# The input projection's weights in two passes instead of four: a hybrid DeltaNet / S5 / HGRN2 layer on one core

## The chip, the cores and the metric

One Trainium2 chip; the kernel runs on one of its cores. The metric is the device time of one execution in microseconds (us), the median of several executions. A core has five engines with queues of their own: TensorE (PE, matmuls; PEld are its weight loads), VectorE (DVE), ScalarE (ACT), GpSimd (POOL) and SyncE (SP, which here issues most DMAs).

## The reference: what is computed

One layer of a hybrid network, in float32, on 2048 prompt tokens and 64 sample tokens (8 sequences of 8), model width 1024:

```python
hn = rmsnorm(h, norm_mix[i])
z = hn @ w_in[i]
z_qkv, z_gate, z_beta, z_a, z_u, z_hq, z_hf, z_hi, z_hg = jnp.split(z, IN_SPLITS, axis=-1)
qkv, buf_qkv = causal_dwconv(z_qkv, conv_qkv[i], dn_conv_w[i])
qkv = jax.nn.silu(qkv).reshape(bsz, t, 3, DN_HEADS, DN_HEAD_DIM)
...
o_a, s_delta = gated_delta_chunked(q, k, v, g, beta, delta[i])
...
y_b, x_re, x_im = s5_ssm(z_u, ssm_re[i], ssm_im[i], ssm_lam_re[i], ssm_lam_im[i], ssm_log_step[i],
...
o_c, s_hg = hgrn2_chunked(hq, hk, hv, jnp.log(f).reshape(hshape), hgrn[i])
...
h = h + jnp.concatenate([o_a, o_b, o_c], axis=-1) @ w_out[i]
hn = rmsnorm(h, norm_ffn[i])
up, buf_ffn = causal_dwconv(hn @ ffn_w_up[i], conv_ffn[i], ffn_conv_w[i])
a_ff, b_ff = jnp.split(up, 2, axis=-1)
h = h + (jax.nn.silu(a_ff) * b_ff) @ ffn_w_down[i]
```

The delta rule works in chunks of 64 tokens with a triangular solve, HGRN2 in chunks of 32 with a state passed from chunk to chunk, S5 is a diagonal scan. A gate, a small projection and a last norm follow; the states are outputs too.

## The kernel before

**Dense products.** Each float32 operand is split into a high part and a low remainder, and one product becomes three matmuls (hi·hi, lo·hi, hi·lo; `mm3`). The tokens are worked in four groups: 512 tokens each, the last one with the 64 sample tokens as well (576). Tiles of 128 tokens are numbered 0 to 15, the sample tile is 16. For each tile `norm_tiles` makes the norm (tile `nx`), transposes it on TensorE and splits it into `hnh` and `hnl` (ScalarE and VectorE); the pair of a group has one of two places, so group 2 takes that of group 0.

**Phase 1**, the input projection (`phase1`), goes group by group. First comes the token unit: for each tile 128 x 264 products for the columns that are wanted by tokens (`tok`). Then come 24 units, one for each block of 128 columns: 12 of qkv, 2 hf, 2 hq, 2 u, 4 zg, 2 hg. A unit is 24 matmuls, 8 steps of 128 rows with three each. It is emptied by `p1_evac`: for qkv two ScalarE copies (`raw`, and `y` with the last tap) and three VectorE steps `y<-raw,cw,y` of the convolution, then a silu on ScalarE and a store.

**The feed** (`Feed`) brings the weights of these units in order: each operand is loaded in two halves (`wr`, by SP), copied by ScalarE to `wh` (the high part) and subtracted to `wl` by GpSimd or VectorE (`split`, whichever is free earlier by the plan). `wh` and `wl` have three places each. `p1_feed` lists for each of the four groups the two token operands and the 24 blocks, so the whole of `w_in` is loaded and split four times, 104 operands.

**Background.** The delta rule (`delta_gen`), S5 and HGRN (`other_gen`) and the norms are Python generators that a class `Background` steps between the dense matmuls (`tick`). When a dense unit needs something that isn't made yet (`need`, `feed.get`), steps are taken by force until it is there. A class `Pace` keeps an estimate of when each engine is free; it only sets the order in which instructions are written. The order on each engine is thereby fixed when the kernel is built. `other_gen` is serial: HGRN of group 0 (two halves of 256 tokens), S5 of groups 0 and 1, HGRN of group 1, HGRN of group 2, S5 of groups 2 and 3, HGRN of group 3. HGRN of a group waits for its token unit and its hf, hq and hg blocks. A half group of HGRN is a load of its rows (`hw`), six doubling levels of small matmuls, transposes, four rounds over chunks with the state `SH`, a norm, and a store to `oT`.

**Phase 3**, the output projection (`phase3`), loads tiles of the mixed outputs back from `oT` as operands of the same feed (`wr<-oT`, split to `wh` and `wl`) against `w_out`, which `load_wo` splits into `woh` and `wol` in the places of the `hn` pairs that are done with. It is called twice; the first part (3a) has tiles 0 to 7, and tile i needs the delta rule, S5 and HGRN of its group. Then come the up projections of the feed-forward part for two groups at a time (phase 4), and the rest. Dense units are numbered through the program: 0 to 136 are phase 1 (group 3's blocks and token tiles count as more than one), and 137 is the first tile of phase 3a.

All instructions are issued by the wrapper `call` of `Pace.Engine`, so every row of the profile has line 71, and rows are told apart by the names of their tiles.

Of the kernel before, what the change touches and what calls it, by code (L numbers as in the profile page):

```python
# [9 lines left out]
F32 = mybir.dt.float32  # L10
# [23 lines left out]
# ranks of background work; how long (us) work of the first rank is waited for; the lead of VectorE over GpSimd  # L34
# [9 lines left out]
class Pace:  # L44
    """An estimate of when each engine gets through what it was given, in microseconds. It serves only to choose the
    order in which independent work is given to the engines."""
# [70 lines left out]
    def keys(ap):  # L117
        """The parts of a tile that ap touches, of those that work goes on in apart."""
# [17 lines left out]
    def ring(self, pool, tag, bufs, ap):  # L136
        """ap takes the place of the tile bufs before it."""
# [65 lines left out]
    def slot(self, what, t, d):  # L203
        """The end of the first gap of d from t on among what is planned."""
# [45 lines left out]
class Background:  # L250
    """Work that runs between the units of the dense products, a step of each at a time, when what the step before
    gave to the engines is done."""
# [8 lines left out]
    def add(self, gen, rank=5):  # L261
        """Generators of the lowest rank come first, and among equals those added first."""
# [4 lines left out]
    def step(self, gen):  # L267
        """The banks that a step of gen took; None when it could not be taken, False after the last."""
# [12 lines left out]
    def tick(self, budget=3, force=False):  # L281
# [13 lines left out]
        if force and not moved:  # L295
            # the first of all before others hold the engines up, then what is ready first
# [8 lines left out]
    def run(self, gen, done):  # L305
        """Steps of gen until done()."""
# [9 lines left out]
class Feed:  # L316
    """The stationary operands of the dense products in the order of their use, loaded and split ahead of it by halves."""

    W = KB * 132

    def __init__(self, m):
        self.m, self.items, self.made, self.raw = m, [], {}, {}
        self.loaded, self.next, self.cur, self.half = 0, 0, 0, None
# [40 lines left out]
    def ahead(self, n):  # L364
        """Steps to the first n operands."""
# [6 lines left out]
    def using(self, i):  # L372
        """Operands before i are in no more use."""
# [4 lines left out]
    def pump(self):  # L378
        """The next step when it holds nothing up."""
# [4 lines left out]
        elif self.next in self.raw and self.next // 2 <= self.cur + 2:  # L384
# [5 lines left out]
    def late(self):  # L390
        """Whether the splits come late and the engines that make them have work to go through."""
        nc = self.m.nc
        lead = {e: nc.free.get(e, 0.0) - nc.now() for e in ("vector", "scalar", "gpsimd")}
        return self.next < 2 * self.cur + 3 and (max(lead["vector"], lead["scalar"]) > 2 or lead["gpsimd"] > 3)

    def get(self, i):
        while self.next < 2 * i + 2:
# [47 lines left out]
class Model:  # L445
# [24 lines left out]
    def split(self, hi, lo, src, lo_eng=None):  # L470
        """hi + lo = src exactly, each in the form that one pass of the tensor engine carries."""
# [32 lines left out]
    def add_rows(self, out, ps, n, x):  # L504
        """out = x + the products of mm_rows."""
# [4 lines left out]
    def rsqrt(self, out, x, n, w, add=0.0):  # L510
        """out = (x + add) ** -0.5 for positive x + add of [n, w], by Newton steps; y takes the other sign in each."""
# [13 lines left out]
    def claim(self, n):  # L525
        """Steps until n of the five banks may be kept from step to step."""
# [12 lines left out]
    def room(self, n):  # L539
        """Steps until a single step may take n banks."""  # L540
# [22 lines left out]
    def masks(self):  # L563
# [11 lines left out]
        # the same within the sequences of the sample tile  # L575
# [17 lines left out]
    def row_bcast(self, dst, src):  # L593
        """A row of DRAM to every partition."""
# [4 lines left out]
    def norm_tiles(self, tiles, source, gain, place, mark, more=(), after={}):  # L599
        """Two generators for the split of (rmsnorm(rows) * gain) transposed, for (tile, group, off, n) of tiles: the  # L600
# [2227 lines left out]
```

## Time and profile before

| | us |
|---|---|
| median of 3 runs (3251.98 to 3255.48) | 3254.16 |
| span of the profiled execution | 3254.1 |
| PE busy | 3086.7 |
| VectorE busy | 1948.4 |
| ScalarE busy | 1246.1 |
| GpSimd busy | 1053.8 |

The span is what the profiler recorded of one execution from its first to its last instruction. An engine's busy time is the sum over its own instructions; the engines work beside each other, so the busy times don't add up to the span. The granted clock (PEclk) is the mean of what TensorE was allowed in a stretch as a share of 2.4 GHz; its lower level is 1.2 GHz. Projection products are `mm`, small background ones `mx`. Phase 1 ends at about 1016 us.

### The profile page before, as it was taken

The page shows a single profiled execution, that of the slowest core. Times are in us where ns is not written, and L with a number is a line of the kernel's source. Part 1 is how long each engine was busy: PE and PEld are TensorE (multiplying, and loading weights), DVE is VectorE, ACT ScalarE, POOL GpSimd, SP SyncE. Part 2 cuts the span into 40 slices and gives each one's busy share as a digit, 9 for nine tenths or more (in the row PEclk, how much of TensorE's full clock was granted, in tenths as well). Part 3 has the DMA queues.
Part 4 walks back from the last instruction along what each step waited for, and adds up shares of the span by engine and source line. Part 5 has one row for each costly group of instructions (what it writes and reads, how often), then busy time and mean ns, then how long its engine had stood idle before and what let it go on. Part 6 is the DMA issues. An engine that isn't in the chain of part 4 may idle for free.

```text
span 3254.1 us, 49953 instructions
## 1 busy us (share of the span) xinstructions
PE 3086.7 (95%) x17872; PEld 2554.5 (78%) x17872; DVE 1948.4 (60%) x4190; ACT 1246.1 (38%) x2920; POOL 1053.8 (32%) x1417
## 2 busy tenths in 40 slices
PE   8898898898898997999999999999999999999998
PEld 6676677687887776777677888999998888888886
DVE  8848859667857579766664446454555323323665
ACT  5454335445453433443243324333334223213333
POOL 4553423534535333134553315343331000000111
PEclk9899999998999998999999999999999999999999
DMA  6465573775467733754242333222225445544221
GB/s 176 132 176 146 140 211 98 203 223 158 130 172 201 224 97 99 202 169 113 80 131 72 97 120 117 63 70 70 67 67 159 135 126 164 148 124 133 73 88 56
DMA packets 627536, 425.52 MB, mean 131 GB/s; under 512 B 112613, under 2 KB 553833, under 8 KB 627016
## 3 DMA queue, kind: packets, MB, share of 16 engines
q1 hardware_dynamic: 596344, 384.24, 41.8%
q10 hardware_dynamic: 30944, 38.09, 3.4%
q8 instruction: 141, 2.31, 0.3%
q14 instruction: 107, 0.88, 0.1%
HBM read 302.69 MB, written 118.95 MB: 130 GB/s over the span
## 4 chain that ended last, share of the span: by engine, by line
PE 59%; DVE 5%; issue 1%; ACT 1%; DMA 1%; POOL 0%; SPq 0%; DVEq 0%; ACTq 0%; POOLq 0%
PE mm L71 53%; PE mx L71 7%; DVE y L71 2%; DVE b L71 1%; DVE R L71 1%; DVE rs L71 1%; DVE s5v L71 0%; SPq L71 0%; DMA b<-xs 0%; DVE s5t L71 0%; ACT djunk L71 0%; POOL s5o L71 0%; ACT y L71 0%; DMA Q<-dNN 0%; DMA dKV<-R 0%
## 5 line engine op out<-in xcount | busy, mean ns | idle before, releaser
L71 PE MATMUL mm<-hnh,wh 128*128 128x512 f32 (+2 forms) x2720 | 994.6, 366 | 20.7 <-ACT wh L71 18.8
L71 PE MATMUL mm<-hnh,wl 128*128 128x512 f32 (+2 forms) x2720 | 992.3, 365 | 17.5 <-POOL wl L71 15.0
L71 PE MATMUL mm<-hnl,wh 128*128 128x512 f32 (+2 forms) x2720 | 993.5, 365 | 0.0
L71 POOL TENSOR_TENSOR wl<-wr,wh 128x512 fp32r<-128x512 f32 (+1 forms) x396 | 564.5, 1434 | 619.8 <-ACT wh L71 604.9
L71 DVE SCALAR_TENSOR_TENSOR y<-raw,fw,y 128x512 f32<-128x512 f32 (+1 forms) x440 | 409.8, 939 | 364.2 <-ACT y L71 290.1
L71 PEld LDWEIGHTS mm<-hnh,wh 128*128 128x128 f32 x2720 | 524.2, 193 | 99.1 <-ACT wh L71 22.6
L71 PEld LDWEIGHTS mm<-hnh,wl 128*128 128x128 f32 x2720 | 523.3, 192 | 98.2 <-POOL wl L71 21.0
L71 PEld LDWEIGHTS mm<-hnl,wh 128*128 128x128 f32 x2720 | 523.5, 192 | 74.7 <-issue 4.9
L71 ACT ACTIVATE wh<-wr 128x512 fp32r<-128x512 f32 (+1 forms) x434 | 265.5, 631 | 161.4 <-PE mm L71 92.1
L71 ACT ACTIVATE raw<-mm 128x512 f32<-128x512 f32 (+3 forms) x336 | 154.8, 461 | 382.8 <-PE mm L71 378.8
L71 PE MATMUL mm<-kh,ghi 128*128 128x512 f32 x748 | 295.1, 394 | 0.5 <-ACT ghi L71 0.3
L71 PE MATMUL mm<-kl,ghi 128*128 128x512 f32 x748 | 294.3, 393 | 0.2 <-DVE kl L71 0.2
L71 PE MATMUL mm<-kh,glo 128*128 128x512 f32 x704 | 277.2, 394 | 0.0
L71 ACT ACTIVATE y<-y 128x512 f32<-128x512 f32 (+1 forms) x136 | 87.7, 645 | 381.4 <-DVE y L71 380.0
L71 ACT ACTIVATE ghi<-kr 128x512 fp32r<-128x512 f32 (+1 forms) x192 | 98.9, 580 | 333.0 <-PE mm L71 284.1
L71 DVE TENSOR_TENSOR h<-mm,h 128x512 f32<-128x512 f32 (+1 forms) x36 | 24.8, 689 | 280.7 <-PE mm L71 280.6
L71 DVE SCALAR_TENSOR_TENSOR y<-raw,cw,y 128x512 f32<-128x512 f32 (+1 forms) x180 | 166.2, 929 | 29.0 <-ACT y L71 17.4
L71 POOL COPY ftail<-raw 128x2 f32<-128x2 f32 x132 | 30.4, 231 | 428.8 <-ACT raw L71 412.1
L71 PEld LDWEIGHTS mm<-kh,ghi 128*128 128x128 f32 x748 | 140.6, 188 | 32.9 <-ACT ghi L71 0.7
L71 PEld LDWEIGHTS mm<-kl,ghi 128*128 128x128 f32 x748 | 140.7, 188 | 32.1 <-DVE kl L71 0.5
L71 PEld LDWEIGHTS mm<-kh,glo 128*128 128x128 f32 x704 | 132.3, 188 | 30.0 <-DVE glo L71 0.4
L71 POOL TENSOR_TENSOR kl<-kr,kh 128x512 fp32r<-128x512 f32 x13 | 17.5, 1350 | 406.8 <-ACT kh L71 396.2
(522 smaller groups left out, 4842.3 us busy)
## 6 DMA issues: line engine op xcount, KB each, us to landing
wr<-in_w_in SPq DMA_DIRECT2D x208, 256.0 KB
wr<-in_ffn_w_up SPq DMA_DIRECT2D x176, 256.0 KB
kr<-gT SPq DMA_DIRECT2D x155, 256.0 KB
gT<-y SPq DMA_DIRECT2D x66, 256.0 KB
h<-h SPq DMA_DIRECT2D x65, 256.0 KB
Q<-zq SPq DMA_DIRECT2D x32, 512.0 KB
wr<-oT SPq DMA_DIRECT2D x48, 256.0 KB
kr<-in_ffn_w_down SPq DMA_DIRECT2D x44, 256.0 KB
```

Source lines behind the costliest of these rows:

```text
L71: return f(*a, **k)
```

## The change

The feed lists the weights twice instead of four times, and `phase1` goes over pairs of groups. For groups (0, 1) and then (2, 3) the units are: the token unit of the first group; then each block of the first group, and, two blocks behind (`LAG`), the same operand used again for the second group; last the token unit of the second group. `wh` and `wl` get four places. Norm tiles get four places in one ring (two and two borrowed ones before). `load_wo` starts all four loads of a half at once and gives the subtractions to GpSimd and VectorE in turn; both halves are queued when group 1 is done and wait for their place.

```diff
 class Feed:
+    BUFS = 4
...
-                self.made[i] = self.items[i][1](*(self.tile(tag, 3) for tag in ("wh", "wl")))
+                self.made[i] = self.items[i][1](*(self.tile(tag, self.BUFS) for tag in ("wh", "wl")))
...
-        elif self.next in self.raw and self.next // 2 <= self.cur + 2:
+        elif self.next in self.raw and self.next // 2 < self.cur + self.BUFS:
...
     def p1_feed(self):
...
-        for g in range(4):
-            for a in range(2):
-                self.feed.add(*tok(a))
-            for _, _, c in self.p1_blocks():
-                self.feed.add(*self.w_block(w, c))
+        for _ in range(2):
+            for _ in range(2):
+                self.feed.add(*tok(0))
+                self.feed.add(*tok(1))
+                if _ == 0:
+                    for _, _, c in self.p1_blocks():
+                        self.feed.add(*self.w_block(w, c))
+
+    LAG = 2
 
     def phase1(self, late, after):
         nc = self.nc
-        for g in range(4):
-            c0, n, blocks, tiles = self.group(g)
...
+        blocks = self.p1_blocks()
+        nb = len(blocks)
+        units = []
+        for ga in (0, 2):
+            at = (nb + 4) * ga // 2
+            units.append((at, ga, None))
+            for x in range(nb + self.LAG):
+                if x < nb:
+                    units.append((at + 2 + x, ga, blocks[x]))
+                if x >= self.LAG:
+                    units.append((at + 2 + x - self.LAG, ga + 1, blocks[x - self.LAG]))
+            units.append((at + 2 + nb, ga + 1, None))
+        self.at = 2 * (nb + 4)
+        for j, (at, g, block) in enumerate(units):
+            self.feed.using(min(u[0] for u in units[j:]))
...
+            self.p1_unit(at, g, block)
...
+            if all(u[1] != g for u in units[j + 1:]):
+                self.flags.add(("p1", g))
+                after(g)
+        self.flush()
+
+    def p1_unit(self, at, g, block):
...
+        kind, b, c = block
+        self.need(*(("hn", i) for i, _, _ in tiles))
+        hi, lo = self.hn[g]
+        wh, wl = self.feed.get(at)
...
+    NX = 4
...
-                if k >= first and done[1] <= (k - first if k < first + 2 else k - 2):
+                if done[1] <= k - self.NX:
                     break
-                if 2 <= k < first:
-                    x = more[k - 2][:n]
-                else:
-                    x = self.np_.tile([128, DM], F32, tag="nx", name="nx", bufs=2)[:n]
+                x = self.np_.tile([128, DM], F32, tag="nx", name="nx", bufs=self.NX)[:n]
...
-            self.split(hi[:, :, c], lo[:, :, c], raws[j])
-            if j < 3:
-                yield (self.nc.when(raws[j + 1]),)
+            self.split(hi[:, :, c], lo[:, :, c], raws[j], (self.nc.gpsimd, self.nc.vector)[j % 2])
         self.flags.add(("wo", half))
...
         def after(g):
-            if g == 2:
-                m.wo = [hn_slot()]
-                m.bg.add(m.load_wo(0, *m.wo[0], ("hn", 16)))
+            if g == 1:
+                m.bg.add(m.load_wo(0, hn_slot(0), ("hn", 16)), 0)
+                m.bg.add(m.load_wo(1, hn_slot(1), ("wo", 0)), 0)
```

`Feed.late` and `Feed.get` also keep the highest operand asked for (`top`), the tiles of phase 3's inputs take the ring of four, and the kernel is built with a smaller scratch room for DMA descriptors.

In numbers, by the order of the instructions: SP issues 128 loads `wr<-in_w_in` instead of 224. ScalarE makes 338 copies to `wh` instead of 434; GpSimd makes 303 subtractions to `wl` instead of 396, VectorE 33 instead of 36. The number of matmuls is the same, 15,709. Ahead of unit 137 stand 1327 background matmuls instead of 1640, ahead of unit 141 1676 instead of 1820.

TensorE's queue at the start, where the third block of group 0 ends; `hnh`, `hnl` are the token operands, `wh`, `wl` the weights, `mx` with `ident` and `nx` are transposes of normalised tiles. Before:

```order
L71 MATMUL mm_730<-hnh_237,wh_641 128x512
L71 MATMUL mm_730<-hnl_238,wh_641 128x512
L71 MATMUL mm_730<-hnh_237,wl_642 128x512
L71 MATMUL mm_801<-hnh_237,wh_740 128x512
L71 MATMUL mm_801<-hnl_238,wh_740 128x512
L71 MATMUL mm_801<-hnh_237,wl_741 128x512
```

and of the changed kernel:

```order
L71 MATMUL mm_823<-hnh_238,wh_684 128x512
L71 MATMUL mm_823<-hnl_239,wh_684 128x512
L71 MATMUL mm_823<-hnh_238,wl_685 128x512
L71 MATMUL mx_895<-ident_83,nx_492 128x128 x4
L71 MATMUL mx_923<-ident_83,nx_492 128x128 x4
L71 MATMUL mx_930<-ident_83,nx_589 128x128 x4
L71 MATMUL mx_958<-ident_83,nx_589 128x128 x4
L71 MATMUL mx_971<-ident_83,nx_710 128x128 x4
L71 MATMUL mx_999<-ident_83,nx_710 128x128 x4
L71 MATMUL mm_1008<-hnh_610,wh_336 128x512
L71 MATMUL mm_1008<-hnl_611,wh_336 128x512
```

Block 3 of the same group followed at once before; now the transposes of three tiles of group 1 stand in a row ahead of group 1's first block, which uses an operand (`wh_336`) of group 0 again.

TensorE's queue at the last chunk round of HGRN for tokens 768 to 1023 (`SH` is its state, `hw` its rows). Before, this stood in phase 1, in a unit of group 3:

```order
L71 MATMUL mm_9324<-hnh_4874,wl_9000 128x256
L71 MATMUL mm_9324<-hnh_4874,wh_8999 128x256
L71 MATMUL mx_9352<-b2_8514,b2_9084 128x128 x2
L71 MATMUL mx_9351<-SH_2043,hw_8511 64x128
L71 MATMUL mx_9351<-b2_8514,b2_8516 64x64 x2
L71 MATMUL mx_9351<-SH_2043,hw_8511 64x128
L71 MATMUL mx_9351<-b2_8514,b2_8516 64x64 x2
L71 MATMUL mm_9324<-hnl_4875,wh_8999 128x256
L71 MATMUL mm_9324<-hnh_4874,wl_9000 128x256
```

and in the changed kernel it stands at the end of 315 background matmuls with no dense one between them, ahead of unit 141, the fifth tile of phase 3a (`woh`):

```order
L71 MATMUL mx_10581<-ident_83,SQ_10493 128x128 x4
L71 MATMUL mx_10586<-R1_10530,KD_10317 128x128 x4
L71 MATMUL mx_10587<-R1_10530,A0_10318 128x128 x4
L71 MATMUL mx_10598<-b2_9986,b2_10420 128x128 x2
L71 MATMUL mx_10597<-SH_2066,hw_9983 64x128
L71 MATMUL mx_10597<-b2_9986,b2_9988 64x64 x2
L71 MATMUL mx_10597<-SH_2066,hw_9983 64x128
L71 MATMUL mx_10597<-b2_9986,b2_9988 64x64 x2
L71 MATMUL mx_10669<-ident_83,b2_10627 128x128 x4
L71 MATMUL mm_10693<-woh_9097,wh_10683 128x512
```

The round moved from between the matmuls of a projection unit to a run without any; the rows with `R1`, `KD` and `SQ` are the delta rule of group 2. In before the longest run without a dense matmul behind the start has 28.

## Rows read from the trace of the kernel before

**Rows 1.** The page's first part: busy us, share of the span, instructions of each engine.

```profile
PE 3086.7 (95%) x17872; PEld 2554.5 (78%) x17872; DVE 1948.4 (60%) x4190; ACT 1246.1 (38%) x2920; POOL 1053.8 (32%) x1417
```

**Rows 2.** Stretches: us, busy PE, PEld, DVE, ACT, POOL (instructions); clock, DMA share, GB/s.

```profile
0.00:250.00 250.00, 210.55 (x1047) 170.90 (x1047) 179.91 (x408) 126.70 (x249) 125.72 (x160) 0.92 0.56 160
250.00:1050.00 800.00, 718.26 (x5411) 604.06 (x5411) 587.77 (x1476) 353.17 (x945) 344.52 (x382) 0.95 0.61 168
```

**Rows 3.** PE's waits up to 1050 us: who ended them; total us, times, longest.

```profile
PE mm L71 <- ACT wh L71: 18.8, 7, 5.8
...
PE mm L71 <- POOL wl L71: 11.2, 12, 2.3
...
PE mx L71 <- DVE nx L71: 8.8, 1, 8.8
...
PE mm L71 <- DVE wl L71: 2.1, 2, 1.9
```

**Rows 4.** Timeline (start, us, engine, operation) around 139 us, and that stretch's table.

```profile
138.00 0.63 ACT L71 ACTIVATE y<-y 128x512 f32<-128x512 f32 x1 [11.32 <-DVE y L71]
...
139.20 0.80 PE L71 MATMUL mm<-hnh,wh 128*128 128x512 f32 x1 [5.82 <-ACT wh L71]
...
143.00 0.40 PE L71 MATMUL mm<-hnl,wh 128*128 128x512 f32 x1
...
130.00:140.00 10.00, 4.18 (x17) 2.94 (x15) 9.66 (x18) 1.99 (x3) 4.69 (x8) 0.81 0.26 92
```

**Rows 5.** Tile `wr` up to 1010 us: times, ns min/median/max, first and last start.

```profile
L71 ACT ACTIVATE wh<-wr x212: 612/630/689, 8.7 to 1000.7; 128x512 fp32r<-128x512 f32 x98, 128x528 fp32r<-128x528 f32 x8
L71 POOL TENSOR_TENSOR wl<-wr,wh x192: 1254/1298/2369, 9.4 to 1009.3; 128x512 fp32r<-128x512 f32 x179, 128x528 fp32r<-128x528 f32 x13
```

**Rows 6.** Timeline of the start: a norm, the first block, a convolution.

```profile
23.32 0.15 DVE L71 TENSOR_TENSOR nss<-nss 128x1 f32<-128x1 f32 x1
...
25.23 1.42 DVE L71 SCALAR_TENSOR_TENSOR nx<-nx,nrs,g_mix 128x512 f32<-128x512 f32 x2
...
36.59 0.40 PE L71 MATMUL mm<-hnh,wh 128*128 128x512 f32 x1
...
51.35 4.14 DVE L71 SCALAR_TENSOR_TENSOR y<-raw,cw,y 128x512 f32<-128x512 f32 x3
```

**Rows 7.** The convolution: grouped by form up to 1050 us, and timeline.

```profile
L71 DVE SCALAR_TENSOR_TENSOR y<-raw,cw,y 128x512 f32<-128x512 f32 x144 | 148.6, 1032 | 28.1 <-ACT y L71 17.4 <-POOL tail L71 5.1 <-POOL cso L71 2.1
...
62.86 2.31 DVE L71 SCALAR_TENSOR_TENSOR y<-raw,cw,y 128x512 f32<-128x512 f32 x3
...
66.98 4.12 DVE L71 SCALAR_TENSOR_TENSOR y<-raw,cw,y 128x512 f32<-128x512 f32 x3 [0.40 <-ACT y L71]
67.49 3.06 POOL L71 TENSOR_TENSOR wl<-wr,wh 128x512 fp32r<-128x512 f32 x2 [0.85 <-ACT wh L71]
```

**Rows 8.** Timeline of one half group of HGRN, 988 to 1062 us (`S`, `Q`: delta rule).

```profile
988.59 0.37 SPq L71 DMA_DIRECT2D oT<-hw  x1
...
995.13 0.99 POOL L71 COPY hw<-hw 128x512 f32<-128x512 f32 x1
...
1005.58 1.56 PE L71 MATMUL mx<-hw 64*64 64x96 f32 x32 [5.66 <-POOL hw L71]
...
1021.91 1.08 PE L71 MATMUL mx<-hw 64*64 64x32 f32 x32
...
1024.81 0.56 PE L71 MATMUL mx<-hw 64*48 64x32 f32 x32
...
1034.38 0.43 PE L71 MATMUL mx<-SH,hw 128*64 128x128 f32 x2
...
1040.80 1.95 PE L71 MATMUL mx<-S,Q 128*128 128x128 f32 x16
...
1047.68 0.43 PE L71 MATMUL mx<-SH,hw 128*64 128x128 f32 x2
...
1061.29 0.75 DVE L71 SCALAR_TENSOR_TENSOR hw<-mx,ghg,hw 128x512 f32<-128x512 f32 x1 [0.36 <-PE mx L71]
```

More of the change, by code (lines that the diff above doesn't have):

```diff
@@ L319 @@
     W = KB * 132
+    BUFS = 4
     def __init__(self, m):
         self.m, self.items, self.made, self.raw = m, [], {}, {}
-        self.loaded, self.next, self.cur, self.half = 0, 0, 0, None
+        self.loaded, self.next, self.cur, self.top, self.half = 0, 0, 0, 0, None
     def add(self, load, view, gate=None):
@@ L393, in late @@
         lead = {e: nc.free.get(e, 0.0) - nc.now() for e in ("vector", "scalar", "gpsimd")}
-        return self.next < 2 * self.cur + 3 and (max(lead["vector"], lead["scalar"]) > 2 or lead["gpsimd"] > 3)
+        return self.next < 2 * max(self.cur, self.top) + 3 and (max(lead["vector"], lead["scalar"]) > 2 or lead["gpsimd"] > 3)
     def get(self, i):
+        self.top = max(self.top, i)
         while self.next < 2 * i + 2:
@@ L596, in row_bcast, with norm_tiles @@
         self.ld(dst, bass.AP(tensor=src.tensor, offset=src.offset, ap=[[0, 128], [1, n]]))
-    def norm_tiles(self, tiles, source, gain, place, mark, more=(), after={}):
+    NX = 4
+    def norm_tiles(self, tiles, source, gain, place, mark, after={}):
         xs, done = {}, [0, 0]
-        first = 2 + len(more)
         def load():
@@ L789, in tok @@
             return load, lambda *x: tuple(v.rearrange("p (k c) -> p k c", k=4) for v in x)
[L791 to L795 removed]
+        for _ in range(2):
[6 more added lines that the diff above has]
+    LAG = 2
     def phase1(self, late, after):
         nc = self.nc
[L799 to L803 removed]
+        blocks = self.p1_blocks()
[13 more added lines that the diff above has]
+            self.feed.using(min(u[0] for u in units[j:]))
+            if j == 0:
                 self.bg.add(late)
                 self.need(("hn", 0))
[L806 removed]
+            self.p1_unit(at, g, block)
+            if j == 0:
+                self.need("setup")
+            if all(u[1] != g for u in units[j + 1:]):
[3 more added lines that the diff above has]
+    def p1_unit(self, at, g, block):
+        nc = self.nc
+        c0, n, blocks, tiles = self.group(g)
+        if block is None:
+            ws = [self.feed.get(at + a) for a in range(2)]
             for j, (i, off, m) in enumerate(tiles):
@@ L826, in phase1 @@
                 self.tick()
-            self.at += 2
-            if g == 0:
-                self.need("setup")
-            for kind, b, c in self.p1_blocks():
-                self.feed.using(self.at)
-                wh, wl = self.feed.get(self.at)
-                for c1, m in blocks:
-                    ps = self.mmbank()
-                    for k in range(8):
-                        self.mm3(ps[:, :m], wh[:, k], wl[:, k], hi[:, k, c1:c1 + m], lo[:, k, c1:c1 + m], k == 0, k == 7, True)
-                        if k < 7:
-                            self.tick()
-                    self.later(ps, lambda a=(g, kind, b, c1, m, ps): self.p1_evac(*a), 6)
-                self.at += 1
-            self.flush()
-            self.flags.add(("p1", g))
-            after(g)
+            return
+        kind, b, c = block
+        self.need(*(("hn", i) for i, _, _ in tiles))
+        hi, lo = self.hn[g]
+        wh, wl = self.feed.get(at)
+        for c1, m in blocks:
+            ps = self.mmbank()
+            for k in range(8):
+                self.mm3(ps[:, :m], wh[:, k], wl[:, k], hi[:, k, c1:c1 + m], lo[:, k, c1:c1 + m], k == 0, k == 7, True)
+                if k < 7:
+                    self.tick()
+            self.later(ps, lambda a=(g, kind, b, c1, m, ps): self.p1_evac(*a), 6)
     def edges(self, raw, taps, first, tail, rows):
@@ L2113, in s5_half, with load_wo @@
             self.st(dst[:, :, SEQ:], ob[:, :, 128:].rearrange("p b c j -> p b (c j)"))
-    def load_wo(self, half, hi, lo, after=None):
+    def load_wo(self, half, slot, after=None):
         if after:
@@ L2168, in pair @@
             if t < 2:
-                return halves(self.np_.tile([128, DM], F32, tag="nx", name="h1x", bufs=2))
+                return halves(self.np_.tile([128, DM], F32, tag="nx", name="h1x", bufs=self.NX))
             if t == 2:
@@ L2690, in tile_hybrid_step, with hn_slot, slot @@
         m.p4_feed()
-        def hn_slot():
-            return [m.hp.tile([128, KB, HN], F32R, tag="hn" + x, name="wo" + x) for x in "hl"]
+        m.wo = {}
+        def hn_slot(half):
+            def slot():
+                yield from m.until(("p1", 2 + half))
+                m.wo[half] = [m.hp.tile([128, KB, HN], F32R, tag="hn" + x, name="wo" + x) for x in "hl"]
+                return m.wo[half]
+            return slot
         def after(g):
-            if g == 2:
-                m.wo = [hn_slot()]
-                m.bg.add(m.load_wo(0, *m.wo[0], ("hn", 16)))
+            if g == 1:
+                m.bg.add(m.load_wo(0, hn_slot(0), ("hn", 16)), 0)
+                m.bg.add(m.load_wo(1, hn_slot(1), ("wo", 0)), 0)
         m.phase1(late(), after)
@@ L2726, in gen, with slot @@
             def gen():
+                def slot(half):
+                    return m.wo[half]
+                    yield
                 for half in range(2):
-                    yield from m.load_wo(half, *m.wo[half])
+                    yield from m.load_wo(half, lambda: slot(half))
                 yield from m.ffn_state()
```

20 lines of the change are left out of this document (6 added, 14 removed).

## The prediction

> **What bounds the kernel now.** I read the engines' busy times first. TensorE is busy 95% of the 3254.1 us span, VectorE 60%, ScalarE 38%, GpSimd 32% [rows 1]. TensorE sets the time, and the change leaves its matmuls alone: the order holds the same 15,709 of them. So only two things can move the time: how long TensorE stands idle, and at which clock it runs. The table by stretches says where that is. Up to 250 us it is busy 210.55 us, from 250 to 1050 us 718.26 us [rows 2]: 39.45 + 81.74 = 121.2 us idle in and just behind the input projection. The granted clock averages 0.92 and 0.95 there, which is 0.08 x 250 + 0.05 x 800 = 60 us of lost full clock. The changed code is all in this stretch.
>
> The table of waits says who ended the idle time there [rows 3]. Projection matmuls that wait for their split weights: 18.8 us for ScalarE's copy `wh`, 11.2 us and 2.1 us for the subtraction `wl` on GpSimd and VectorE, 32.1 us together. The very start: 8.8 us for the first normalised tile. The rest, 121.2 - 32.1 - 8.8 = 80.3 us, are nearly all background matmuls (`mx`) that wait for vector work. The stage where the split weights come late shows a second price: after a wait of 5.82 us at 139.20 the matmuls take 0.80 us each until the 0.40 us at 143.00 [rows 4]. The ten microseconds around it have a granted clock of 0.81 [rows 4], a mean of the 1.2 and 2.4 GHz levels. Some 3.5 us at half pace lose 1.75 us for 5.82 us idle, 0.3 for one. Over the whole stretch it is 60/121 = 0.5. I take 0.4: an idle microsecond costs 1.4.
>
> **T1, the split weights.** The feed holds 104 operands before and 56 after, so 48 operands, or 96 halves, fall away: 96 loads, 96 copies of 0.630 us on ScalarE and 96 subtractions, almost all of 1.298 us on GpSimd [rows 5]. That is 60 us of ScalarE and about 120 us of GpSimd, none of it on the path by itself; only the 32.1 us of waits are. Two units now share an operand, so each has twice the time for its split, and the ring is four deep instead of three. I take 26 of the 32 us as gone: 26 x 1.4 = **-36**. Bounds: all of it at the whole stretch's factor, 32 x 1.5 = -48; and -10, because the longest wait stays possible. At 138.00 ScalarE had stood 11.32 us behind a silu that waited for VectorE [rows 4], and the `wh` copy stood behind that silu in its queue. Fewer splits don't shorten that queue; only the deeper ring helps.
>
> **T2, the start.** Group 1 now starts after three blocks of group 0, and a block needs all four token tiles of its group normalised and transposed. In the order of PE six groups of transposes (tiles 5 to 7) stand in a row with no dense matmul between them. Before, block 0 began at 36.59 and block 1's convolution, right behind its product, at 51.35 [rows 6], so the third block ends near 57. VectorE spends 3.3 us on the norm of a tile (23.32 to 26.65), 4.14 us on each convolution [rows 6] and two subtractions of some 0.7 us on each transposed tile. Behind the fourth tile's share for group 0, four tiles cost 4 x (3.3 + 1.4) = 19 us, three convolutions 12 us, and the norms of tiles 8 to 10, which now lie in between since four buffers are free, another 10. From about 31 us that gives 72, so 15 us idle: x 1.4 = **+21**. Bounds +5 (the norms ahead of the first blocks, convolution late) and +30.
>
> **T3, the other background waits.** Ahead of phase 3's fifth tile stood 1820 background matmuls; now 1676, of which 315 stand in one run (T4). So 459 fewer lie between dense matmuls there. At 80.3/1640 = 0.049 us each (1640 stood in phase 1) that is -22 us; 144 of them come later and pay +7. VectorE gains too: a convolution step takes 1032 ns on average, while three take 2.31 us (0.77 each) without GpSimd work beside them and 4.12 us with the subtractions of 67.49 beside them [rows 7]. With half the subtractions gone, 144 x 0.26 / 2 = 18 us of VectorE time come free; I take 6 us of idle for it. Sum -21 x 1.4 = **-29**. Bounds -42 and 0: TensorE may simply wait for VectorE at other places.
>
> The Trainium skill ("SBUF — State Buffer", section "SBUF: two separate sides") says that a VectorE instruction with two SBUF inputs and a GpSimd instruction that reads SBUF exclude each other from a shared pair of ports, the later one blocking. By that rule the convolutions would go to 0.77 us wherever a subtraction is gone, and the trace agrees: 4.12 against 2.31 us. It would be worth the whole 18 us, which is the third rival.
>
> **T4, the stretch without dense work.** HGRN of group 0 needs its last blocks and the token operand of the group, and group 1's token unit now stands at the end of the pass. So HGRN starts near unit 50 instead of 30. Tile 4 of the output projection needs HGRN of group 1. Before, that had long been done. Now, behind unit 140, PE's order has 315 background matmuls and not one dense: the whole second half of group 1, and the delta states of group 2 beside it. How long is that chain? The trace shows the same chain for a later half group: result of the half before stored at 988.59, first use of the next rows 995.13, first matmul 1005.58, levels to 1034.38, chunk rounds to 1047.68, result behind its norm at 1061.29 [rows 8]. From 988.59 to its end at 1062.04 it is 73.5 us. Standing alone it should be shorter: 10.4 us before the first matmul, where GpSimd and VectorE had other work, become 3; the levels' 28.8 become 24 (one level is 2.9 us, 1021.91 to 1024.81 [rows 8], six are 17, plus transposes); the rounds' 13.3 become 12. That leaves 60. Behind it stand the store, the load back and the split, 7.7 us (a store and a load took 6.5 from 988.59 to 995.13; a copy of 0.63 and a subtraction follow). 68 us, less 3 that begin before the last dense matmul: 65. TensorE's own work in it: 84 wide matmuls at 1.95/8 = 0.24 us [rows 8] and 231 narrow ones at 0.06 us (1.08 us for 16 of them [rows 8]) = 34 us. So 31 us idle, and 5 for the clock: **+36**. Bounds: +25 with all levels at 2.9 us, +58 with the chain at its full 73.5 + 7.7 us.
>
> The Trainium skill ("TensorE: Matmul & The Clock Gate", Part 1: The HAM clock gate) speaks against the change here: the default state is throttled, and activity releases it. In a stretch of narrow matmuls the granted clock would then be 1.2 GHz. The trace shows such a thing only in small: 0.81 around 139, and half pace after one wait [rows 4].
>
> All else has one answer: fewer weight loads come free (no projection matmul shows a DMA as the thing waited for), the `w_out` splits by GpSimd and VectorE in turn and the larger norm ring have no wait before that they could remove, and phases 4 to 6 stay as they are, since the background has ended in both.
>
> **Sum.** -36 + 21 - 29 + 36 = -8. On the profiled 3254.1, which is the median 3254.16 but for 0.06, that is **3246 us**.
>
> **The rivals.** *The stretch decides, slower* (0.32). T4's chain is serial; if it doesn't shorten at all, T4 is +58 and the sum +14, 3268; with T2 at +30 and T3 at half it is 3291. The clock can do the same: if half of the 34 us lies on the chain and runs at half pace, as the matmuls behind 139.20 did [rows 4], that is +17, 3263. The rule of the Trainium skill above would bring that about. The point from which it decides: the chain over 73 us instead of 65, with all else as forecast. For it: every step is a round trip between TensorE and VectorE, and the delta states share the engines. Against it: those same steps had dense matmuls in front of them in the trace. *Nothing to measure* (0.21): the four terms cancel within 6.5 us, which is 0.2% of the time and about what a measurement can tell from no change. 3248 to 3260. *VectorE's relief is worth it all* (0.17): 18 us instead of 6, T3 = -42, and T1 -44: 3225. *The change does not do what it says* (under 0.01): the order has 128 loads of `w_in` instead of 224.
>
> **How the numbers follow.** The forecast's own case, a small gain of 7 to 20 us, has 0.30, and with VectorE's relief faster has 0.47; same 0.21; slower 0.32. The bounds add up, each side as root of squares, to -26 and +45 around -8: 3220 to 3291. I take 3219 to 3287.
>
> **What would show it.** T1: waits for `wh` and `wl` below 10 us up to 1050. T2: one PE wait of 10 to 20 us near 57 to 75 us, ended by `hnl`. T3: the convolution's mean near 0.9 us. T4: near 1000 us a stretch of 55 to 75 us in which PE has no `mm`, half busy. Wrong it would be if the stretch is longer than 75 us, or if the waits for `wh` only turn into waits of `mx` for VectorE.

## The result and the profile after

The changed kernel takes 3197.85 us (median of 4 runs, 3197.67 to 3199.41) against 3254.82 of the kernel before beside it: a ratio of 0.9825, with an interval of 0.9814 to 0.9836. That is 57 us, where 8 were forecast, and below the range. The profiled span is 3195.9 us, 58.2 less than before. Two runs below each have one execution of over twice the usual time (6749.42 us with the norms held back, 7565.57 us with the token unit earlier); their medians here leave it out, and as the second run's profile fell on it, no row of that run is shown.

The first part of the page of after (busy us, share of the span, instructions), beside [rows 1]:

```profile
PE 3059.7 (96%) x17872; PEld 2541.0 (80%) x17872; DVE 1882.4 (59%) x4195; ACT 1196.0 (37%) x2823; POOL 899.9 (28%) x1316
```

TensorE has the same 17,872 instructions but is busy 27.0 us less. Most of that is the clock: laid over TensorE's busy time, the trace's records of the granted clock have 135 us at the lower level before and 90 after, which at half pace is 22.6 us less lost. The idle part went from 3254.1 - 3086.7 = 167.4 to 136.2 us, 31.2 less. The second surprise is VectorE: its work is the same but for a few subtractions, yet it is busy 66 us less.

Where this happened is seen in a table by stages: the first 100 us, the rest of phase 1, phase 3a, phase 4. First the kernel before (columns as in [rows 2]: us, busy PE, PEld, DVE, ACT, POOL, clock, DMA share, GB/s):

```profile
0.00:100.00 100.00, 80.67 (x388) 67.34 (x389) 81.29 (x204) 50.82 (x106) 43.82 (x68) 0.91 0.57 166
100.00:1016.00 916.00, 815.68 (x5753) 683.78 (x5752) 668.04 (x1634) 415.68 (x1062) 407.02 (x454) 0.94 0.59 163
1016.00:1158.40 142.40, 138.32 (x1020) 108.75 (x1019) 77.63 (x213) 60.07 (x167) 57.40 (x48) 0.99 0.78 223
1158.40:1959.90 801.50, 770.28 (x4155) 604.02 (x4154) 517.90 (x1085) 296.29 (x674) 286.67 (x452) 0.98 0.40 116
```

and the changed kernel:

```profile
0.00:100.00 100.00, 69.32 (x318) 57.82 (x319) 83.69 (x242) 45.38 (x105) 31.98 (x65) 0.88 0.53 158
100.00:898.00 798.00, 760.28 (x5217) 651.15 (x5216) 559.00 (x1416) 356.73 (x896) 265.66 (x332) 0.98 0.54 154
898.00:1088.70 190.70, 160.72 (x1202) 130.88 (x1200) 116.25 (x338) 68.19 (x205) 65.36 (x63) 0.87 0.58 171
1088.70:1901.50 812.80, 787.69 (x4576) 613.01 (x4575) 519.80 (x1144) 303.44 (x706) 281.99 (x462) 0.99 0.40 116
```

| stage | idle before | idle after | change |
|---|---|---|---|
| first 100 us | 19.3 | 30.7 | +11.4 |
| rest of phase 1 | 100.3 | 37.7 | -62.6 |
| phase 3a | 4.1 | 30.0 | +25.9 |
| phase 4 | 31.2 | 25.1 | -6.1 |

Phase 1 lost 62.6 us of idle time and ran at a clock of 0.98 instead of 0.94. It is 118 us shorter, part of it work that moved behind it; phase 3a gave 48 back and phase 4 another 11.

The waits that answer to [rows 3], up to 1050 us of the changed kernel (who ended them; us, times, longest):

```profile
PE mm L71 <- ACT wh L71: 7.7, 3, 5.9
...
PE mm L71 <- POOL wl L71: 0.6, 1, 0.6
```

8.3 us where 32.1 were. The convolution, grouped by form up to 1050 us, beside [rows 7], and a small step of the delta rule's norms, the same group in both kernels (changed, then before):

```profile
L71 DVE SCALAR_TENSOR_TENSOR y<-raw,cw,y 128x512 f32<-128x512 f32 x144 | 139.3, 967 | 39.2 <-ACT y L71 22.5 <-POOL cso L71 7.0 <-DMA s_to<-s_ht 2.4
...
L71 DVE TENSOR_TENSOR rs<-rs 128x8 f32<-128x8 f32 x96 | 18.8, 196 | 3.3
```

```profile
L71 DVE TENSOR_TENSOR rs<-rs 128x8 f32<-128x8 f32 x102 | 31.5, 309 | 3.5
```

The convolution gained 9.3 us in all. The other 57 of the 66 us are spread over everything else that VectorE does; a step on 128 x 8 elements fell from 309 to 196 ns.

The start and the stretch without dense work, on PE's timeline of the changed kernel (start, us, operation, idle time and what ended it), and the stretch's row, columns as in the tables above:

```profile
63.79 0.40 PE L71 MATMUL mm<-hnh,wl 128*128 128x512 f32 x1
...
69.20 0.66 PE L71 MATMUL mx<-ident,nx 128*128 128x128 f32 x4 [3.70 <-ACT mx L71]
...
74.54 1.97 PE L71 MATMUL mx<-ident,nx 128*128 128x128 f32 x8 [4.67 <-DVE hnl L71]
...
76.34 0.79 PE L71 MATMUL mm<-hnh,wh 128*128 128x512 f32 x1
...
927.54 0.40 PE L71 MATMUL mm<-woh,wl 128*128 128x512 f32 x1
...
1003.69 0.80 PE L71 MATMUL mm<-woh,wh 128*128 128x512 f32 x1 [5.95 <-ACT wh L71]
```

```profile
927.50:1003.70 76.20, 53.77 (x613) 46.10 (x612) 43.84 (x159) 20.75 (x93) 13.06 (x19) 0.74 0.41 113
```

From 63.79 to 76.34 no dense matmul runs, only the transposes of group 1. From 927.54 to 1003.69, 76 us, there is none either: that is the run of 315 background matmuls, in which TensorE is busy 53.77 us and idle 22.4. Both matmuls behind a gap take 0.8 us, half pace.

### The profile page after: what moved, and what is told of

The parts are those of the page before. It is cut to its first block, busy times and chain, and to the rows that moved or that the text cites. A ratio compares the mean times of both kernels' runs of the same rounds, so it can differ in the third digit from the quotient of the medians.

```text
span 3195.9 us, 49480 instructions
## 1 busy us (share of the span) xinstructions
PE 3059.7 (96%) x17872; PEld 2541.0 (80%) x17872; DVE 1882.4 (59%) x4195; ACT 1196.0 (37%) x2823; POOL 899.9 (28%) x1316
## 4 chain that ended last, share of the span: by engine, by line
PE 57%; DVE 3%; DMA 1%; issue 1%; ACT 1%; SPq 1%; POOL 0%; DVEq 0%; ACTq 0%; POOLq 0%
PE mm L71 51%; PE mx L71 6%; DVE y L71 1%; SPq L71 1%; DVE R L71 1%; DVE b L71 0%; DVE s5v L71 0%; DVE rs L71 0%; POOL wl L71 0%; DMA b<-xs 0%; DMA kr<-gT 0%; DMA wr<-in_ffn_w_up 0%; DMA fs_rows<-in_state_conv_ffn 0%; ACT b L71 0%; ACT raw L71 0%
## 5 line engine op out<-in xcount | busy, mean ns | idle before, releaser
L71 PE MATMUL mm<-hnh,wh 128*128 128x512 f32 (+2 forms) x2720 | 980.1, 360 | 9.7 <-ACT y L71 9.7
L71 PE MATMUL mm<-hnl,wh 128*128 128x512 f32 (+2 forms) x2720 | 982.3, 361 | 4.1 <-DVE hnl L71 4.1
L71 PE MATMUL mm<-hnh,wl 128*128 128x512 f32 (+2 forms) x2720 | 980.2, 360 | 0.0
L71 PEld LDWEIGHTS mm<-hnh,wh 128*128 128x128 f32 x2720 | 516.7, 190 | 85.1 <-ACT y L71 11.0
L71 PEld LDWEIGHTS mm<-hnl,wh 128*128 128x128 f32 x2720 | 516.2, 190 | 78.7 <-issue 4.8
L71 PEld LDWEIGHTS mm<-hnh,wl 128*128 128x128 f32 x2720 | 516.6, 190 | 73.7 <-issue 4.7
L71 POOL TENSOR_TENSOR wl<-wr,wh 128x512 fp32r<-128x512 f32 (+1 forms) x303 | 429.4, 1428 | 476.3 <-ACT wh L71 463.5
L71 ACT ACTIVATE wh<-wr 128x512 fp32r<-128x512 f32 (+1 forms) x338 | 204.9, 633 | 139.4 <-PE mm L71 61.7
L71 DVE SCALAR_TENSOR_TENSOR y<-raw,cw,y 128x512 f32<-128x512 f32 (+1 forms) x180 | 153.5, 858 | 40.0 <-ACT y L71 22.5
L71 ACT ACTIVATE y<-mm,fw 128x512 f32<-128x512 f32 (+2 forms) x220 | 133.7, 608 | 5.6 <-DVE y L71 5.0
```

The lines of the kernel that those rows point to most:

```text
L71: return f(*a, **k)
```

## Experiments

Two theories were set against each other for the gain of phase 1 beyond the waits for the weights. **A, relief:** a subtraction on GpSimd holds VectorE up, and 96 fewer of them let everything that waits for VectorE come earlier. **B, order:** the background is spread thinner, since part of it moved behind phase 1. The first three kernels, and the one with copies made twice, keep every queue in the order of their parent and change only what is named; in the others the plan orders the background anew.

**96 subtractions more.** In the changed kernel, behind the split of each block half:

```diff
             (nc.vector if dve + 0.6 < pool + 1.2 - LEAN else nc.gpsimd).tensor_sub(lo, part, hi.bitcast(F32))
+            i = self.next // 2
+            if i < 56 and 2 <= i % 28 < 26:
+                a, b = (self.m.g_mix[:, x:x + 512].rearrange("p (k c) -> p k c", k=4) for x in (0, 512))
+                nc.gpsimd.real.tensor_sub(part, a, b)
```

> The changed kernel, every queue in the same order, with 96 more subtractions on GpSimd (two inputs, 128x512, behind the split of each half of the 48 weight blocks; no matmul waits for them). Theory A (relief of VectorE: what phase 1 gained beyond the waits for the weights is VectorE working 66 us less because fewer GpSimd subtractions run beside it): VectorE's busy time goes from 1882 back to about 1940 us and the time from 3198 to 3220 to 3245 us. Theory B (the new order: the background is spread thinner and moved behind phase 1): below 3205 us, whatever VectorE's busy time does.

Measured: 3275.73 us, ratio to before 1.0066 (1.0048 to 1.0084), so 78 us more than the changed kernel, above both ranges expected. The page's first part:

```profile
PE 3076.8 (94%) x17872; PEld 2551.5 (78%) x17872; DVE 1948.3 (60%) x4195; ACT 1197.3 (37%) x2823; POOL 1034.4 (32%) x1412
```

VectorE is back at 1948.3 us, the number of before, with no instruction of its own added. Its instructions' durations, added up by operation, are 64 us longer: `SCALAR_TENSOR_TENSOR` 43.2 and `TENSOR_TENSOR` 17.4, which take two tensors, and all others together 3.5. The loss lies where the subtractions were added: the rest of phase 1 takes 875.3 us instead of 798.0, phase 3a 187.7 instead of 190.7. TensorE is idle 3268.9 - 3076.8 = 192.1 us instead of 136.2. The waits for `wh` and `wl` up to 1050 us are 1.5 and 4.3 us, not more than the 8.3 of the changed kernel, so the 78 us are background waits and clock. Theory A said 22 to 47 us and was too small; B is out as the source of the gain, since the new order is kept and the gain is gone. The subtraction writes into the raw weights' buffer, so the next load waits for it; the control is the next run, which does that too.

**288 memsets more,** at the same places and into the same buffer:

```diff
+            i = self.next // 2
+            if i < 56 and 2 <= i % 28 < 26:
+                for _ in range(3):
+                    nc.gpsimd.real.memset(part, 0.0)
```

> The changed kernel, same order, with 3 x 96 memsets of 128x512 on GpSimd at the same places (0.524 us each, 151 us in all, which only write). Theory A with the cause in GpSimd's reading beside VectorE's: VectorE's busy time stays within 10 us of 1882 and the time at 3198 to 3206 us. If it is GpSimd's queue being full that counts, the same loss as with the 96 subtractions, 3220 us or more. Theory B: 3198 to 3205 us.

Measured: 3233.2 us, 0.9935 (0.9918 to 0.9951), 35 us more than the changed kernel. The page's first part, and the group of the memsets (busy us, mean ns; they are issued past the wrapper, so their line is 365):

```profile
PE 3067.5 (95%) x17872; PEld 2547.2 (79%) x17872; DVE 1881.6 (58%) x4195; ACT 1197.8 (37%) x2823; POOL 1044.5 (32%) x1604
```

```profile
L365 POOL MEMSET wr<- 128x512 f32 x288 | 152.9, 532 | 16.2
```

GpSimd is busier than with the subtractions (1044.5 against 1034.4 us), but VectorE is at 1881.6, as in the changed kernel. So two costs lie on top of each other, and neither expectation had both. GpSimd's time and the later loads cost 35 us; TensorE is idle 160.1 us instead of 136.2, though its waits for `wh` and `wl` (7.4 and 0.6 us up to 1050) are those of the changed kernel. Reading beside VectorE is left with the rest, 78 - 35 = 43 us, if the queue and the loads cost as much under the subtractions as under the memsets. How the 35 divide into GpSimd's queue and the loads wasn't tried.

**Before, without 96 subtractions.** In groups 1 and 3 the low parts of the blocks are left out, and the third matmul takes the high part:

```diff
-            (nc.vector if dve + 0.6 < pool + 1.2 - LEAN else nc.gpsimd).tensor_sub(lo, part, hi.bitcast(F32))
+            i = self.next // 2
+            e = nc.vector if dve + 0.6 < pool + 1.2 - LEAN else nc.gpsimd
+            if i < 104 and i // 26 % 2 and i % 26 >= 2:
+                nc.note(e, "tensor_sub", (lo, part, hi.bitcast(F32)), {})
+            else:
+                e.tensor_sub(lo, part, hi.bitcast(F32))
...
-        mm(ps, ll, rh, start=False, stop=stop)
+        if fake:
+            self.nc.note(self.nc.tensor, "matmul", (ps, ll, rh), {})
+            self.nc.tensor.real.matmul(ps, lh, rh, start=False, stop=stop)
+        else:
+            mm(ps, ll, rh, start=False, stop=stop)
...
```

> The kernel before, same order, without the low parts of the weights of the 24 blocks in groups 1 and 3: their 96 subtractions are left out (87 on GpSimd, 9 on VectorE) and the third matmul takes the high part in the low part's place; loads, copies and the number of matmuls stay. Theory A: VectorE's busy time falls from 1948 to about 1890 us, the waits of phase 1 by 40 to 60 us, and the time is 3195 to 3220 us. Theory B: only the waits for the low parts go, some 7 of 13 us, times 1.4: 3240 to 3248 us.

Measured: 3206.73 us, 0.9858 (0.9841 to 0.9874): 49 us gained in the order of before. The page's first part:

```profile
PE 3068.9 (96%) x17872; PEld 2543.7 (79%) x17872; DVE 1885.3 (59%) x4181; ACT 1246.5 (39%) x2920; POOL 931.0 (29%) x1330
```

VectorE is busy 63 us less here as well, of which its own 9 subtractions left out are 8 us; the other 55, over 87 subtractions of GpSimd, are 0.63 us each. TensorE is idle 3204.2 - 3068.9 = 135.3 us instead of 167.4, 32 less. The waits for `wh` did not fall (18.8 before, 23.0 here), those for `wl` fell by 5 us, so 31 of the 32 us are other waits. Theory A's forecast of the time holds and B's (3240 to 3248 us) doesn't. This run takes work off GpSimd's queue as well as off VectorE, so it can't tell the two apart; only the two runs before it do.

**Two operands.** The order of units of the changed kernel, but each unit loads and splits for itself (the list of the feed changes to match):

```diff
-            units.append((at, ga, None))
+            at = (2 * nb + 4) * ga // 2
+            units.append((at, ga, None))
+            at += 2
             for x in range(nb + self.LAG):
                 if x < nb:
-                    units.append((at + 2 + x, ga, blocks[x]))
+                    units.append((at, ga, blocks[x]))
+                    at += 1
                 if x >= self.LAG:
-                    units.append((at + 2 + x - self.LAG, ga + 1, blocks[x - self.LAG]))
+                    units.append((at, ga + 1, blocks[x - self.LAG]))
+                    at += 1
...
```

> The changed kernel with its order of units, but each unit loads and splits an operand of its own (224 loads of the input weights instead of 128; 192 block halves split instead of 96). Theory A: what was gained in phase 1 goes, the stretch without dense work stays: 3245 to 3275 us. Theory B: only the waits for split weights come back, 24 us x 1.4: 3220 to 3235 us.

Measured: 3296.71 us, 1.0129 (1.0114 to 1.0145), above both ranges expected. This takes the change apart: the new order, with four places for `wh` and `wl`, costs 3296.7 - 3255.8 = 41 us, and sharing the operands gives 99 back. In the terms of the sum, the order has T2, T4 and the moved background of T3, 21 + 36 - 21 = +36, and sharing has T1 and VectorE's relief, -36 - 8 = -44. So sharing was forecast at less than half. And the waits for `wh` and `wl` up to 1050 us are 15.3 us here, against 32.1 before and 8.3 in the changed kernel: 17 us of that fall need no sharing. Counted with the order, at 1.4, they make the forecast +12 for the order and -20 for sharing, and then both were too small. The background's own steps fall differently here (the run without dense work is 62.5 us long, not 76), so the split is rough.

**Copies twice.** Of the 99 us the subtractions explain 78. ScalarE's part was tried by making each of the 96 copies twice:

```diff
             nc.scalar.activation(hi, part, AF.Copy)
+            if i < 56 and 2 <= i % 28 < 26:
+                nc.scalar.real.activation(hi, part, AF.Copy)
```

> The changed kernel, same order, with each of the 96 ScalarE copies of the weight blocks made twice (0.63 us each, 60 us of ScalarE). The kernel with an operand for each unit stood 99 us above the changed one, the one with 96 more GpSimd subtractions 78 us. If ScalarE's copies make the rest, 10 to 25 us: 3208 to 3223 us. If they are hidden: 3196 to 3203 us.

Measured: 3204.64 us, 0.9837 (0.9821 to 0.9854). The interval overlaps that of the changed kernel; 60 us of ScalarE cost some 7 us, if anything. The copies are a small part at most; the 96 loads weren't tried by themselves.

**All subtractions on VectorE.** One line, `or self.next < 112` in the choice of the engine:

> The changed kernel with all subtractions of the input projection's weights on VectorE (0.7 us each alone) instead of mostly on GpSimd (1.3 us). If a subtraction on GpSimd costs VectorE 66/96 = 0.69 us anyway, VectorE's busy time stays within 20 us of 1882 and the time is 3185 to 3210 us. If GpSimd's subtractions were nearly free for VectorE: its busy time is 60 us longer and the time over 3225 us.

Measured: 3229.32 us, 0.9921 (0.9907 to 0.9936). VectorE's busy time is 1863.2 us, 19 less than in the changed kernel, though it does 90 subtractions more. Its own subtractions take 64 us more and all its other work 83 less, so a subtraction costs VectorE at least as much from outside as from inside. The time is 31 us longer all the same, and not the 3185 to 3210 us expected, so busy time alone does not decide. Phase 1 is not what became slower: its rest takes 792.0 us with 30.6 idle, against 798.0 and 37.7. The first 100 us have 38.1 us of idle time instead of 30.7; behind the matmul at 13.04 us TensorE waits 9.04 us for `wl`, a subtraction that stands in VectorE's queue. The rest lies in phase 3a:

```profile
892.00:1106.60 214.60, 168.54 (x1290) 135.53 (x1289) 131.73 (x392) 63.71 (x179) 69.14 (x72) 0.79 0.49 143
```

46.1 us idle at a clock of 0.79, with a run without dense work of 83 us. TensorE waits 28.1 us there for GpSimd's steps on `hw`, against 1.8 in the changed kernel. The plan orders the background anew in this run; how much of the 31 us comes from the place of the subtractions in VectorE's queue is not shown.

**Blocks of HGRN earlier.** To take away the run of 315: the blocks in the order qkv, hf, hq, hg, u, zg.

```diff
-        l = [("qkv", b, C_QKV + 128 * b) for b in range(12)]
-        for kind, c, n in (("hf", C_HF, 2), ("hq", C_HQ, 2), ("u", C_U, 2), ("zg", C_ZG, 4), ("hg", C_HG, 2)):
+        l = []
+        for kind, c, n in (("qkv", C_QKV, 12), ("hf", C_HF, 2), ("hq", C_HQ, 2), ("hg", C_HG, 2), ("u", C_U, 2), ("zg", C_ZG, 4)):
```

> The changed kernel with the blocks of the input projection in another order: qkv, hf, hq, hg, u, zg (hg was last), so that HGRN of the first group of a pair can start some six blocks (twelve units) earlier. The order of PE then has no run of over 28 background matmuls ahead of phase 4; the run of 315 is gone. If the run costs what its stage shows (26 us of idle time and 23 us of lost clock in phase 3a): 3150 to 3165 us. If the background's work is then only in the way in phase 1: 3185 us or more.

Measured: 3189.04 us, 0.9795 (0.9776 to 0.9815), 9 us better; the interval just touches that of the changed kernel. Its stages (rest of phase 1, 3a, 4):

```profile
100.00:932.70 832.70, 790.11 (x5744) 668.81 (x5742) 570.00 (x1491) 359.97 (x948) 290.30 (x365) 0.98 0.54 151
932.70:1057.10 124.40, 107.70 (x625) 85.39 (x624) 91.01 (x222) 42.53 (x90) 56.93 (x49) 0.92 0.56 166
1057.10:1893.80 836.70, 807.53 (x4620) 634.19 (x4619) 530.59 (x1170) 317.95 (x765) 287.12 (x458) 0.98 0.43 124
```

Phase 3a is 66 us shorter and the run is gone. But phase 1 is 35 us longer and phase 4 24. Most of that is work that moved; idle time went from 30.0 to 16.7 in 3a and rose by 5 and 4 in the others, 4.6 us less over the whole kernel. My expectation took the stage's excess for the price of the run. It was wrong: most of the waits went along with the work.

**Blocks of HGRN first,** hf, hq, hg, qkv, u, zg:

> The changed kernel with the blocks in the order hf, hq, hg, qkv, u, zg. HGRN can start after six blocks, the delta rule six blocks later, and the first blocks have no convolution on VectorE while it still normalises. No run of over 44 background matmuls. If the run and the start are what holds the changed kernel up: 3140 to 3160 us, the gap at 64 to 76 us shorter. If the delta rule starts too late: over 3170 us, with a run of its matmuls ahead of phase 3a.

Measured: 3199.82 us, 0.983 (0.9815 to 0.9845): no gain, with phase 3a at 121.4 us, but phase 1 ending only at 967.6. The time is in the second range expected, but the run of the delta rule's matmuls named with it is not there: behind the start the longest stretch without dense work is 12.6 us.

**Less ahead of phase 3a,** qkv, u, hf, hq, hg, zg:

> The changed kernel with the block order qkv, u, hf, hq, hg, zg: no run of over 28 background matmuls either, but 1467 of them ahead of phase 3a against 1603 with hg behind hq, 1501 against 1624 ahead of its fifth tile. If crowding in phase 1 is what keeps the gain of the block order small: 3175 to 3186 us. If the waits only move with the work: 3187 to 3200 us.

Measured: 3200.96 us, 0.9825 (0.9805 to 0.9844). Less background in phase 1 did not help: TensorE is idle 3202.7 - 3057.2 = 145.5 us, against 131.6 with hg behind hq.

**Norms held back.** For the gap at 64 us:

```diff
-                while k not in xs:
+                while k not in xs or mark == "hn" and k >= 8 and ("hn", 7) not in self.flags:
```

> The changed kernel with the norms of tiles 8 and on held back until group 1's tiles are transposed. If the gap of 12.6 us at 64 to 76 us comes from norms of later tiles in VectorE's queue, it falls to 3 to 6 us and the time by 8 to 12 us, to 3186 to 3190 us. If the four tiles' own norms set it, it stays and so does the time, 3195 to 3202 us.

Measured: 3252.51 us, 0.9991 (0.998 to 1.0002), 55 us worse, which neither expectation had. The gap shrank from 12.6 to 8.8 us, so about a third of it was the later tiles' norms. But every plan behind it changed, and the run ahead of the fifth tile of phase 3a is the worst of all: on PE's timeline no dense matmul starts from 921.51 to 1038.97, 117 us. The stage's row:

```profile
884.40:1138.60 254.20, 192.53 (x1525) 152.76 (x1524) 157.62 (x488) 73.74 (x232) 72.57 (x80) 0.77 0.49 142
```

61.7 us idle at a clock of 0.77.

**Both together,** the norms held and the blocks of HGRN earlier:

> The changed kernel with the block order qkv, hf, hq, hg, u, zg and the norms of tiles 8 and on held back. Holding the norms took 4 us off the gap at 64 to 76 us but cost 55 us by moving HGRN further back, with a run of 300; here no run of over 28 background matmuls is left. If the run made that loss: 3175 to 3190 us. If held norms cost by themselves: 3200 us or more.

Measured: 3184.82 us, 0.9783 (0.9766 to 0.9799). With the norms held, the order of the blocks is worth 68 us; without, 9. Phase 3a goes from 254.2 to 135.5 us and from 61.7 to 10.8 us of idle time, and the whole kernel from 180.3 to 130.1: here nearly all the idle time that left the stage stays away, where with the shorter run of 76 us 4.6 of 13.3 did. So the loss of the run before it was the long run, not the norms. This kernel is 13 us below the changed one, and the intervals lie apart.

**Token unit earlier,** the second group's token unit ahead of block 18, with the same order of blocks:

> The changed kernel with the block order qkv, hf, hq, hg, u, zg and the token unit of the second group ahead of block 18 instead of at the end of its pass (its two operands loaded there). HGRN of the odd group can start earlier. No run of over 28 background matmuls; 1640 of them ahead of phase 3a as before the change. If an earlier HGRN helps beyond the run: 3170 to 3185 us. If it only crowds phase 1: 3186 to 3200 us.

Measured: 3184.15 us, 0.9781 (0.9763 to 0.98): 5 us below the order of the blocks alone (3189.04), with intervals that overlap, so no gain of its own is shown.

## Why the prediction was wrong

**T1, waits for the split weights: right in size.** In the rest of phase 1 they were 13.5 + 10.6 + 2.1 = 26.2 us and are gone; up to 1050 us they fell by 24 where 26 were forecast. With an operand for each unit they fell by 17 already, so most of it needed no sharing.

**T2, the start.** 15 us of idle time were forecast, 11.4 measured (16 without the 5 us of waits for split weights that went there), the gap at 64 to 76 us instead of 57 to 72, in two waits of 3.70 and 4.67 us instead of one. The cause named was right in part: the norms of later tiles made 4 of the 12.6 us.

**T4, the stretch: seen, its clock too small.** It was 76 us long where 65 were forecast, beyond the 73 us at which the first rival was to decide and the 75 us that were to show the prediction wrong. TensorE is busy 53.77 us in it instead of 34, at a clock of 0.74, and idle 22.4 instead of 31. Over phase 3a the idle time rose by 25.9 us. The stage's mean clock of 0.87 is 25 us of lost clock, but part of that lies in idle time, where a low clock costs nothing: laid over TensorE's busy time it is 17.1 us against 1.7 before, 15 more where 5 were forecast. Idle and clock together are +41 instead of +36, inside the bounds. The Trainium skill ("TensorE: Matmul & The Clock Gate", Part 1: The HAM clock gate) says that the default state is throttled and that activity releases it. This trace agrees in part: the 0.74 of the stretch is a mean of both levels and not 1.2 GHz throughout. The first rival had this stretch right, and yet the kernel did not become slower, because of T3.

**T3, the other waits: the step that failed.** Take T1, T2 and T4 from the -31.2 us of idle: -26.2 + 11.4 + 25.9 = +11.1, so T3 is -42 us, twice the -21 of the sum (a remainder, in which the -6.1 of phase 4 lie too). What failed is the price of the 96 subtractions beyond the waits for their results, and it was set too low at two places.

First, VectorE's relief: "With half the subtractions gone, 144 x 0.26 / 2 = 18 us of VectorE time come free; I take 6 us of idle for it." It counted the convolutions alone, since their rows had shown the effect, and then took a third of it. Measured are 9.3 us at the convolutions but 66 us over all of VectorE's work, and the runs with 96 subtractions more and 96 fewer give 66 and 63. A subtraction of some 1.4 us on GpSimd takes 0.69 us from VectorE on average.

Second, GpSimd's own time: T1 has "about 120 us of GpSimd, none of it on the path by itself". The memsets, 153 us on GpSimd that don't lengthen VectorE's work, cost 35 us of time all the same (with the loads that they delay), 24 us of it idle, with no more waits for split weights. The rows of before held a sign of it: of the 80.3 us that the prediction put down to "vector work", GpSimd's results ended 18 (among them 9.5 on `hw` and 4.2 on `KD`).

Both together are seen without the new order in the kernel before with 96 subtractions fewer: 31 us of idle time beyond the waits for the weights, where the sum had 6. The other part of T3, the background moved out of phase 1 (-22 + 7), was not tested by itself.

The third rival (relief is worth it all, 3225 us) had VectorE's part of the mechanism and the same size of 18 us, and so it fell short too.

**The clock: too small a factor.** 0.4 us were taken for each idle one. Laid over busy time, the lost clock of the rest of phase 1 fell from 46.3 to 14.2 us, 32 for 62.6 us of idle: 0.5. In phase 3a it was 15 for 25.9, 0.6. Over the kernel it is 22.6 for 31.2, 0.7, of the 27.0 us of busy time that went.

In one line: idle -1 forecast and -31 measured, busy time -7 and -27. Of the 30 us missing in idle, 21 are T3, 5 are T4's and 4 are T2's.

## What to carry to other kernels

When a change takes work off GpSimd, price it on VectorE too: multiply the number of instructions that go by what one takes from VectorE, over all that VectorE does, not over the rows in which it was first seen. Price GpSimd's own queue as well, even where no dense matmul is seen to wait for it. A wait that a change adds or removes at one place is worth its whole stage only where nothing else waits at the place it moves to; the way to know is to take it away. Where the clock is below full speed, idle time and lost clock move together, here by 0.5 to 0.7 us of clock for one of idle, and the lost clock is to be counted over TensorE's busy time alone.

## What the runs showed of the hardware

- A GpSimd subtraction with both inputs in SBUF takes 0.69 us from VectorE on average (96 of them: 1882.4 to 1948.3 us of VectorE's busy time, same instructions), and 61 of the 64 us by which the durations grew are in VectorE operations with two tensor inputs. Memsets of more GpSimd time take nothing (1881.6). The Trainium skill ("SBUF — State Buffer", section "Who interferes with whom") says that VectorE instructions with two SBUF inputs contend with GpSimd instructions that read SBUF and not with those that only write; the two runs agree.
- That GpSimd pays as well is not shown: where it has 96 subtractions more, the median of its subtractions to `wl` is 1.308 us, and 1.305 in the changed kernel.
- Not expected was how much it weighs on the whole: 96 subtractions cost 78 us of 3200, and no matmul waits for their results.
